# A layer with product-key experts: key rows from a second, transposed copy of peer_u instead of transposes on TensorE

## Chip, cores and metric

The kernel runs on one core of a Trainium2 chip. The metric is the device time of one execution in microseconds; lower is better. Engines are named PE (TensorE), DVE (VectorE), ACT (ScalarE), POOL (GpSimd) and SP (SyncE, which issues most DMAs).

## What is computed

One layer over 1024 latent tokens of width 1024 with 256 context tokens: a modulated norm, an input projection, retention beside differential attention, an output projection, and then a PEER layer, in which every token retrieves experts by product keys. The change lies in the last:

```python
def block_fn(hb):
    q = (hb @ w_query).reshape(t, 8, 2, 128)
    s = einsum('thpc,hpnc->thpn', q, sub_keys)
    v1, i1 = top_k(s[:, :, 0], 16); v2, i2 = top_k(s[:, :, 1], 16)
    cand = v1[..., :, None] + v2[..., None, :]
    best, pos = top_k(cand, 16)                     # 16 of 256 pairs, for each of 8 heads
    experts = i1 * 128 + i2                         # at pos: 128 experts per token, of 16384
    gate = softmax(best)
    act = gelu(einsum('thkd,td->thk', expert_u[experts], hb))
    return einsum('thk,thkd->td', gate * act, expert_v[experts])
```

All data are float32.

## The kernel before

**Two ways through the experts.** The 8 blocks of 128 tokens are split. Blocks 0 to 3 are *gathered*: for each of a token's 128 experts POOL issues an indirect DMA that fetches one 4 KB row of `peer_u` or `peer_v` per token into a `gat` tile (four buffers). `u_step` (from L1212) multiplies the row with the token's h2 on DVE and keeps the sum as a coefficient; `v_step` (L1224) multiplies the row by its coefficient and adds it to `acc` on DVE, or for some ranks scales it on ACT and adds it to `acp` on POOL. That makes 512 u gathers and 512 v gathers. In `halves` (L1208) the u rows of one half block alternate with the v rows of the half before, so that the last 64 v rows come alone.

Blocks 4 to 7 (512 tokens, `DENSE`) take the *dense* part: all 16384 experts for all tokens, with gates that are zero for those not retrieved. `dense_phase` (L1371) goes through 128 key rows of 128 experts, in groups of four. For a key row, `dense_act` (L1315) forms the coefficients: it loads the 128x1024 rows of `peer_u` into `uraw` (tag `wst`, four buffers), transposes them on PE in eight pieces of 128x128 (L1326), and splits the result into a high and a low half, `uh` and `ul` (tag `h`): ACT casts to float32r (L1328) and DVE subtracts what the cast kept from the original (L1329). Three float32r matmuls per piece of the width then give the product with the tokens, which were split in the same way (tags `k` and `v`). After a gelu and the gate (tags `k`, `aT`), the coefficients are split too, and `dense_val` (L1350) multiplies them with the rows of `peer_v` (tag `sel`), whose split has the tags `vi` (cast on ACT) and `pt` (subtraction, on DVE for two of three and on POOL for the third). A group's results are added to `dacc` (tag `b`) on DVE. PSUM has eight banks, all of tag `mm`.

**What sets the order.** No order is written out by hand. `Plan.record` (L208) keeps every instruction with its dependencies, `Plan.cost` (L259) gives it an estimated duration, and `Plan.schedule` (L289) orders all with a list schedule: by priority, and by whether a tile's tag has a free buffer. A priority is the PE time planned so far. `Plan.weave` (L186) sorts several recorded parts together by their position in the list, and `dense_phase` is woven with the last block's selection. The gathers have priorities of their own, a start (`POFF`) and steps per gather (`PACES`), in the same planned PE time:

```python
pr = f0 + POFF
for i, _ in enumerate(halves()):
    nc.prio = pr
    pr += [p for lo, p in PACES if i >= lo][-1]
```

The planned order is then fixed on each engine, and an engine waits for whatever is next in it. Since all instructions are issued from one line (L448), the rows below go by the tiles' names.

Of the kernel before, what the change touches and what calls it, by code (L numbers as in the profile page):

```python
# [14 lines left out]
D = 1024  # L15
# [28 lines left out]
TG = 32  # L44
# [15 lines left out]
class View:  # L60
    """A part of a planned tile: the steps that lead to it, replayed on the real tile when it is traced."""
# [79 lines left out]
class Plan:  # L141
    """Records the kernel's instructions with their data dependencies, orders them with a list schedule on
    estimated durations, and traces them in that order; Tile then places every wait."""
# [35 lines left out]
    def capture(self, fn, *a):  # L179
        """the instructions of fn as a list for weave()"""  # L180
        self._log = log = []
        fn(*a)
        self._log = None
        return log

    def weave(self, *parts):  # L186
        """records captured lists side by side; a part is (list, from, to) with from, to in 0..1"""
        keyed = []
        for x, (log, lo, hi) in enumerate(parts):
            last, key = None, 0.0  # L190
            for j, it in enumerate(log):
                if it[4] is None or it[4] is not last:
                    key = lo + (hi - lo) * j / max(1, len(log))
                last = it[4]
                keyed.append((key, x, j, it))
        keyed.sort(key=lambda z: z[:3])
        for _, _, _, (eng, meth, a, k, u) in keyed:
            if u is None:
                self._in_unit = False
            elif u is not self._token:  # L200
                self._in_unit, self._unit = True, None
            self._token = u
            self.record(eng, meth, a, k)
        self._in_unit, self._unit, self._token = False, None, None
# [84 lines left out]
    def schedule(self):  # L289
# [36 lines left out]
        def blocked(n):  # L326
            """the tag for which the node's tiles have no slot yet, or None"""
            need = {}
            for b in fresh(n):
                need.setdefault(b.tag, []).append(pos[id(b)])  # L330
            for t, ps in need.items():
                bs = self.order[t]
                while head[t] < len(bs) and id(bs[head[t]]) in taken:
                    head[t] += 1
                first = max(ps) < head[t] + len(ps)
                if free[t] < len(ps) + (0 if first else self.reserve.get(t, 99)):
                    return t
            return None
# [116 lines left out]
def layer(tc, I, out, dbg=None):  # L455
# [3 lines left out]
    with sp as S, pp as P, dp as DR:  # L459
# [41 lines left out]
        def rstd(dst, mean):  # L501
            """dst = (mean + eps) ** -0.5 on a narrow tile"""
            n = mean.free
            nc.vector.tensor_scalar(dst, mean, EPS, None, op0=OP.add)
            nc.gpsimd.tensor_tensor(out=dst, in0=dst, in1=mhalf[:, :n], op=OP.pow)

# [82 lines left out]
        def split_cols(kb, xt, tags):  # L589
            """a block's normed, modulated tokens as columns, split in two"""  # L590
# [32 lines left out]
        # log gamma = min(x, 0) - log1p(exp(-|x|)), with log1p(e) = log(u) + (e - (u - 1)) / u, u = 1 + e  # L623
# [15 lines left out]
        # decay columns: [.., a, kind, h], a = forward / backward, kinds k, q, ctx block 0, ctx block 1  # L639
# [17 lines left out]
        # lambda of the differential softmax  # L657
# [9 lines left out]
        # rope tables with the norms' gains in them  # L667
# [13 lines left out]
        def rope(dst, src, cos, sin, g):  # L681
            """dst = src * cos + rot(src) * sin for g groups of 64; src may lie in PSUM"""
# [24 lines left out]
        def three(pm, ah, al, bh, bl, first, last):  # L707
            """pm += (ah + al)^T (bh + bl), each a float32 split in two; the product of the two low parts is below
            float32's last place"""
            nc.tensor.matmul(pm, ah, bh, start=first, stop=False)  # L710
            nc.tensor.matmul(pm, ah, bl, start=False, stop=False)
            nc.tensor.matmul(pm, al, bh, start=False, stop=last)
# [3 lines left out]
        def project3(c0, hs, fn):  # L716
            """256 columns of the input projection, of split tokens"""
# [102 lines left out]
        def late_queries(blocks, tag="rv"):  # L820
            """queries and retention gates of blocks"""
# [11 lines left out]
        # R[:, c] is the state before chunk c in scan order: rows 0:64 forward, rows 64:128 backward  # L833
# [18 lines left out]
        def head_norm(dst, src, gain):  # L852
            """rms over each 128 of 512 columns, times the gain; src in SBUF"""
# [98 lines left out]
        def sub_keys():  # L952
            """the product keys, transposed"""
# [81 lines left out]
        def mix(grp):  # L1035
            """token mixers, output projection and the second norm of up to two blocks; returns h2 of each"""
# [76 lines left out]
        def split_tokens():  # L1113
            """h2 of the dense blocks, transposed and split"""
# [16 lines left out]
        def select(b, v16, i16):  # L1131
# [49 lines left out]
            # per pair of head and rank, on partitions: rows of the two halves' keys and the gate  # L1181
# [26 lines left out]
        def halves():  # L1208
            """the gathered blocks' rows, by half blocks: u rows of one half beside v rows of the half before"""
# [57 lines left out]
        def gates(b):  # L1267
            """gate of expert (i1, i2) for each token of a dense block, into Wd[t // TG][i2][i1][t % TG]; the one-hot
            rows of i1 are products of one-hots of its upper and lower part, those of i2 are relu(1 - |index - column|)"""
# [45 lines left out]
        def dense_act(hhl, i1, wt, j, cs):  # L1315
            """coefficients of the experts of key row i1, for all dense tokens"""
            uraw = sb([128, D], "wst")
            nc.sync.dma_start(uraw, u2[i1 * 128:(i1 + 1) * 128, :])
            uh = sb([128, KD, 128], "h", F32R)
            ul = sb([128, KD, 128], "h", F32R)  # L1320
            for g in range(2):
                tp = ps([128, 4, 128])
                with nc.unit():
                    for q in range(4):
                        k = g * 4 + q
                        nc.tensor.transpose(tp[:, q, :], uraw[:, k * 128:(k + 1) * 128], ident)  # L1326
                ks = slice(g * 4, g * 4 + 4)
                nc.scalar.copy(uh[:, ks, :], tp)  # L1328
                nc.vector.tensor_tensor(out=ul[:, ks, :], in0=tp, in1=uh[:, ks, :].bitcast(F32), op=OP.subtract)  # L1329
# [138 lines left out]

_INS = ["x", "c", "ctx", "c_ctx", "w_mod", "b_mod", "norm1_g", "norm2_g", "w_in", "ret_decay_logit", "ret_norm_g",
# [17 lines left out]
```

## Time and profile before

| | |
|---|---|
| runs (3), median | 3866.08 us (3861.67 to 3867.92) |
| the profiled execution: span from the first to the last instruction | 3853.5 us |
| the profiled execution's own time | not listed apart; it lies among runs whose median is 12.6 us above the span |
| PE, PE weight loads | 3169.3 us (82%), 2518.7 us (65%) |
| DVE | 3019.1 us (78%) |
| ACT | 1429.2 us (37%) |
| POOL | 2283.8 us (59%) |
| moved by DMA | 917.87 MB, 238 GB/s |

Busy times of engines overlap, and a share of the whole span mixes stages: projections and attention in the first half, the dense part beside the gathers in the second. For a change in one stage, the table of that stage (busy times in a stretch), the waits in it, and the chain that ended last say more.

### The profile page before, as it was taken

How to read it: one execution, taken by the hardware profiler on the slowest of the kernel's cores; microseconds unless marked ns; L12 is line 12 of the kernel's file. 1: busy time of each engine (PE TensorE's matmuls, PEld its weight loads, DVE VectorE, ACT ScalarE, POOL GpSimd, SP SyncE). 2: the span in 40 equal slices, each digit the busy share in tenths (PEclk: the TensorE clock that was granted, in tenths of full speed). 3: DMA queues.
4: the chain of work that ended last, by engine and by line, in shares of the span. 5: the costliest groups of instructions: out<-in, count | busy, mean ns of one | idle time of the engine just before them, and what ended most of it. 6: DMA issues, size and time to landing. Idle time of an engine off the chain costs nothing. (4 is left out here: it accounts for less than half of the span.)

```text
span 3853.5 us, 46264 instructions
## 1 busy us (share of the span) xinstructions
PE 3169.3 (82%) x15209; PEld 2518.7 (65%) x15209; DVE 3019.1 (78%) x5843; ACT 1429.2 (37%) x3316; POOL 2283.8 (59%) x1744
## 2 busy tenths in 40 slices
PE   7999998788778658857588898888898888988884
PEld 5998675666556536646476676666677667766663
DVE  3456457788999998999977887787888777778785
ACT  4332424243255447756532233222222222222221
POOL 0111114556765665655677777776777776666677
PEclk9999997889879768867699999999999999999997
DMA  5324464967557657867778888788898888788786
GB/s 179 94 67 130 131 204 148 321 234 248 193 175 253 221 183 238 303 224 245 241 254 286 285 277 274 259 277 279 284 304 292 279 292 277 269 273 274 266 280 214
DMA packets 427392, 917.87 MB, mean 238 GB/s; under 512 B 33384, under 2 KB 224400, under 8 KB 427152
## 3 DMA queue, kind: packets, MB, share of 16 engines
q0 software_dynamic: 147456, 536.94, 41.0%
q1 hardware_dynamic: 279696, 377.98, 29.6%
q8 instruction: 120, 1.97, 0.2%
q14 instruction: 120, 0.98, 0.1%
HBM read 861.84 MB, written 52.95 MB: 237 GB/s over the span
## 5 line engine op out<-in xcount | busy, mean ns | idle before, releaser
L448 DVE SCALAR_TENSOR_TENSOR gat<-gat,h2t 128x1024 f32<-128x1024 f32 x512 | 787.3, 1540 | 177.2 <-DMA gat<-peer_u,egb 174.6
L448 PE MATMUL mm<-k,h 128*128 128x512 f32 x2048 | 748.1, 423 | 142.4 <-DVE h L448 125.1
L448 POOL DMA_INDIRECT gat<-peer_v,egb x512 | 633.3, 1237 | 391.1 <-DVE acc L448 197.4
L448 POOL DMA_INDIRECT gat<-peer_u,egb x512 | 590.6, 1153 | 397.4 <-DVE gat L448 188.5
L448 DVE SCALAR_TENSOR_TENSOR acc<-gat,act,acc 128x1024 f32<-128x1024 f32 x365 | 571.2, 1565 | 111.8 <-DMA gat<-peer_v,egb 111.0
L448 PEld LDWEIGHTS mm<-k,h 128*128 128x128 f32 x2048 | 403.7, 200 | 261.2 <-DVE h L448 150.8
L448 PE MATMUL mm<-v,h 128*128 128x512 f32 x1024 | 421.2, 411 | 0.0
L448 POOL TENSOR_TENSOR acp<-acp,gat 128x1024 f32<-128x1024 f32 x139 | 340.2, 2447 | 64.8 <-ACT gat L448 62.3
L448 PE MATMUL mm<-vi,t 128*128 128x512 f32 x1024 | 355.4, 411 | 0.0
L448 PE MATMUL mm<-vi,rv 128*128 128x512 f32 x1024 | 353.0, 406 | 0.2 <-DVE b L448 0.2
L448 PE MATMUL mm<-o,t 128*128 128x128 f32 x1024 | 201.7, 353 | 177.1 <-DVE o L448 125.9
L448 POOL TENSOR_TENSOR m<-m,mhalf 128x4 f32<-128x4 f32 (+1 forms) x78 | 82.6, 1061 | 406.6 <-DVE m L448 397.8
L448 PEld LDWEIGHTS mm<-o,t 128*128 128x128 f32 x1024 | 174.0, 251 | 214.1 <-issue 60.3
L448 ACT CAST vi<-sel 128x512 fp32r<-128x512 f32 x256 | 158.5, 621 | 389.3 <-PE mm L448 331.0
L448 PE MATMUL mm<-b,wst 128*128 128x256 f32 (+1 forms) x1280 | 266.3, 368 | 3.4 <-ACT t L448 1.7
L448 PE MATMUL mm<-pt,t 128*128 128x512 f32 x512 | 215.4, 421 | 63.0 <-POOL pt L448 32.7
L448 ACT ACTIVATE gat<-gat,act 128x1024 f32<-128x1024 f32 x139 | 160.0, 1151 | 287.0 <-DMA gat<-peer_v,egb 226.7
L448 PE MATMUL mm<-pt,rv 128*128 128x512 f32 x512 | 212.9, 416 | 58.7 <-DVE pt L448 32.5
L448 PEld LDWEIGHTS mm<-b,wst 128*128 128x128 f32 x1280 | 226.1, 213 | 38.9 <-issue 5.2
L448 PEld LDWEIGHTS mm<-vi,t 128*128 128x128 f32 x1024 | 202.5, 198 | 47.2
L448 PEld LDWEIGHTS mm<-v,h 128*128 128x128 f32 x1024 | 204.4, 200 | 42.8
L448 PEld LDWEIGHTS mm<-vi,rv 128*128 128x128 f32 x1024 | 199.6, 195 | 45.3 <-issue 0.4
(249 smaller groups left out, 6620.8 us busy)
## 6 DMA issues: line engine op xcount, KB each, us to landing
wst<-peer_u SPq DMA_DIRECT2D x128, 512.0 KB
sel<-peer_v SPq DMA_DIRECT2D x256, 256.0 KB
wst<-peer_w_query SPq DMA_DIRECT2D x80, 512.0 KB
Wd<-rv SPq DMA_DIRECT2D x64, 512.0 KB
h<-Wd SPq DMA_DIRECT2D x64, 512.0 KB
wst<-w_mod SPq DMA_DIRECT2D x48, 512.0 KB
wst<-w_out SPq DMA_DIRECT2D x40, 512.0 KB
wst<-w_in SPq DMA_DIRECT2D x32, 512.0 KB
```

Of the source, the lines that this page charges most:

```text
L448: getattr(handles[n.eng], meth)(*[res(v) for v in a], **k)
```

## The change

The host adds an input, `peer_u_cols`: for each key row the 128 experts' vectors with the width on the partitions, so that a key row arrives as it left the transposes before. `uraw` is loaded from it, and `uh` and `ul` are made from it in one operation each, of 128x1024 from SBUF in place of two each of 128x512 from PSUM. Matmuls, tags, buffer counts and the planner's constants (`POFF`, `PACES` and the others) stay as they are. The gathers still read `peer_u`.

```diff
         def dense_act(hhl, i1, wt, j, cs):
-            uraw = sb([128, D], "wst")
-            nc.sync.dma_start(uraw, u2[i1 * 128:(i1 + 1) * 128, :])
+            uraw = sb([128, KD, 128], "wst")
+            nc.sync.dma_start(uraw, I["peer_u_cols"][i1])
             uh = sb([128, KD, 128], "h", F32R)
             ul = sb([128, KD, 128], "h", F32R)
-            for g in range(2):
-                tp = ps([128, 4, 128])
-                with nc.unit():
-                    for q in range(4):
-                        k = g * 4 + q
-                        nc.tensor.transpose(tp[:, q, :], uraw[:, k * 128:(k + 1) * 128], ident)
-                ks = slice(g * 4, g * 4 + 4)
-                nc.scalar.copy(uh[:, ks, :], tp)
-                nc.vector.tensor_tensor(out=ul[:, ks, :], in0=tp, in1=uh[:, ks, :].bitcast(F32), op=OP.subtract)
+            nc.scalar.copy(uh, uraw)
+            nc.vector.tensor_tensor(out=ul, in0=uraw, in1=uh.bitcast(F32), op=OP.subtract)
             pm = ps([128, ND])
...
+def host_layouts(inputs):
+    u = np.asarray(inputs["peer_u"])[0].reshape(128, 128, KD, 128)
+    return {"peer_u_cols": np.ascontiguousarray(u.transpose(0, 3, 2, 1))}
...
     arrays.update(shape_constants())
+    arrays.update(host_layouts(inputs))
```

Since the planner sees other steps, it writes another order from the first key row on. On DVE in the middle of the stage, where `h` rows are u splits, `k` and `aT` rows the gating of a key row's coefficients, `gat` and `acc` rows gathers, `pt` rows v splits and `b` rows the sums, the queue read before:

```order
L448 SCALAR_TENSOR_TENSOR gat,act<-gat,h2t 128x1024
L448 TENSOR_TENSOR h<-mm,h 128x512 x3
L448 SCALAR_TENSOR_TENSOR acc<-gat,act,acc 128x1024
L448 TENSOR_TENSOR h<-mm,h 128x512
L448 SCALAR_TENSOR_TENSOR gat,act<-gat,h2t 128x1024
L448 TENSOR_TENSOR pt<-sel,vi 128x512 x2
L448 SCALAR_TENSOR_TENSOR acc<-gat,act,acc 128x1024
L448 TENSOR_TENSOR h<-mm,h 128x512
L448 SCALAR_TENSOR_TENSOR gat,act<-gat,h2t 128x1024 x2
L448 TENSOR_TENSOR k<-k,h 128x256 x2
L448 TENSOR_TENSOR aT<-aT,h 128x256 x2
```

and a like piece of it now:

```order
L448 SCALAR_TENSOR_TENSOR gat,act<-gat,h2t 128x1024
L448 TENSOR_TENSOR h<-wst,h 128x1024
L448 TENSOR_TENSOR k<-k,h 128x256 x2
L448 SCALAR_TENSOR_TENSOR gat,act<-gat,h2t 128x1024
L448 TENSOR_TENSOR h<-wst,h 128x1024
L448 SCALAR_TENSOR_TENSOR acc<-gat,act,acc 128x1024
L448 SCALAR_TENSOR_TENSOR gat,act<-gat,h2t 128x1024
L448 TENSOR_TENSOR aT<-aT,h 128x256 x2
L448 TENSOR_TENSOR pt<-sel,vi 128x512 x2
L448 TENSOR_TENSOR h<-wst,h 128x1024
```

A key row's split is one row instead of two, and splits of several rows stand together: counted over the 128 key rows, a row's split stands on average 2.6 key rows ahead of the gating on DVE, before 1.6. Between two splits there are fewer gathers.

At the end of DVE's queue stood before:

```order
L448 TENSOR_TENSOR pt<-sel,vi 128x512
L448 SCALAR_TENSOR_TENSOR acc<-gat,act,acc 128x1024 x3
L448 TENSOR_TENSOR b<-b,mm 128x512 x2
L448 SCALAR_TENSOR_TENSOR acc<-gat,act,acc 128x1024
L448 TENSOR_TENSOR b<-b,mm 128x512
L448 SCALAR_TENSOR_TENSOR acc<-gat,act,acc 128x1024
L448 TENSOR_TENSOR b<-b,mm 128x512
```

and now:

```order
L448 SCALAR_TENSOR_TENSOR gat,act<-gat,h2t 128x1024 x2
L448 SCALAR_TENSOR_TENSOR acc<-gat,act,acc 128x1024
L448 SCALAR_TENSOR_TENSOR gat,act<-gat,h2t 128x1024
L448 SCALAR_TENSOR_TENSOR acc<-gat,act,acc 128x1024
L448 SCALAR_TENSOR_TENSOR gat,act<-gat,h2t 128x1024
L448 TENSOR_TENSOR act<-act,egb 128x64
L448 SCALAR_TENSOR_TENSOR acc<-gat,act,acc 128x1024 x51
```

Dense work (`pt`, `b`) stood to the last; now the queue ends in gathers alone. Behind DVE's last `b` row there are 19 multiplies of u gathers and 66 accumulations of v gathers. In POOL's queue no gather stood behind the last `pt` split, and now 104 of the 1024 do; the dense blocks' closing operations on POOL (`b<-b,wst`) stand among those.

## Rows read from the trace of the kernel before

**Rows 1.** The page: span; busy us of each engine, share of the span, instructions

```profile
span 3853.5 us, 46264 instructions
...
PE 3169.3 (82%) x15209; PEld 2518.7 (65%) x15209; DVE 3019.1 (78%) x5843; ACT 1429.2 (37%) x3316; POOL 2283.8 (59%) x1744
```

**Rows 2.** Busy by stretch: PE, weight loads, DVE, ACT, POOL, granted clock, DMA share, GB/s

```profile
1885.00:3813.00 1928.00, 1665.70 (x7161) 1311.65 (x7161) 1532.71 (x1855) 551.32 (x880) 1396.49 (x1006) 0.94 0.82 277
```

**Rows 3.** Waits, 1885 to 3813: who waited for whom, us in total, times, longest

```profile
POOL gat L448 <- DVE acc L448: 151.7, 98, 5.5
POOL gat L448 <- DVE gat L448: 151.3, 110, 3.7
...
PE mm L448 <- DVE h L448: 125.1, 47, 13.8
...
POOL gat L448 <- issue: 91.0, 337, 0.6
...
PE mm L448 <- DVE pt L448: 62.3, 32, 6.8
PE mm L448 <- POOL pt L448: 55.7, 33, 6.1
```

**Rows 4.** Tile `gat`, 1885 to 3860: count, ns min/median/max, first and last start

```profile
L448 POOL DMA_INDIRECT gat<-peer_v,egb x376: 935/1118/2016, 1892.0 to 3812.9; - x188
L448 DVE SCALAR_TENSOR_TENSOR gat<-gat,h2t x315: 1208/1225/5019, 1889.7 to 3649.9; 128x1024 f32<-128x1024 f32 x158
...
L448 POOL DMA_INDIRECT gat<-peer_u,egb x313: 935/959/2007, 1886.5 to 3639.6; - x157
L448 DVE SCALAR_TENSOR_TENSOR acc<-gat,act,acc x278: 1267/1282/4328, 1894.7 to 3820.9; 128x1024 f32<-128x1024 f32 x139
```

**Rows 5.** Tiles `wst`, `h` and `pt` in the stage, columns as in the group above

```profile
L448 PEld LDWEIGHTS mm<-ident,wst x1024: 137/141/231, 1885.6 to 3747.8; 128*128 128x128 f32 x171
...
L448 DVE TENSOR_TENSOR h<-mm,h x256: 673/680/697, 1904.0 to 3748.8; 128x512 fp32r<-128x512 f32 x128
...
L448 DVE TENSOR_TENSOR pt<-sel,vi x170: 673/684/4014, 1912.0 to 3808.6; 128x512 fp32r<-128x512 f32 x170
```

**Rows 6.** The page's chain that ended last: share of the span by line

```profile
DMA gat<-peer_v,egb 5%; PE mm L448 4%; POOL gat L448 4%; DMA gat<-peer_u,egb 4%; POOL acp L448 2%; DVE gat L448 1%; POOL pt L448 1%; DVE acc L448 1%; POOL t L448 1%; POOL rv L448 1%; DVE h L448 0%; DVE b L448 0%; POOL b L448 0%; POOL acc L448 0%; ACT gat L448 0%
```

**Rows 7.** Timeline of PE's loads around four transposes: start us, us

```profile
2832.24 0.59 PEld L448 LDWEIGHTS mm<-ident,wst 128*128 128x128 f32 x4
2832.79 0.19 PEld L448 LDWEIGHTS mm<-k,h 128*128 128x128 f32 x1
```

**Rows 8.** Groups by line and form: busy us, mean ns of one, idle before it

```profile
L448 DVE SCALAR_TENSOR_TENSOR gat<-gat,h2t 128x1024 f32<-128x1024 f32 x315 | 519.6, 1650 | 142.7 <-DMA gat<-peer_u,egb 140.1 <-POOL pt L448 1.6 <-issue 0.4
...
L448 DVE SCALAR_TENSOR_TENSOR acc<-gat,act,acc 128x1024 f32<-128x1024 f32 x275 | 434.6, 1580 | 104.0 <-DMA gat<-peer_v,egb 103.2
...
L448 DVE TENSOR_TENSOR h<-mm,h 128x512 fp32r<-128x512 f32 x256 | 169.9, 682 | 24.9 <-ACT h L448 23.5 <-issue 1.0
L448 DVE TENSOR_TENSOR pt<-sel,vi 128x512 fp32r<-128x512 f32 x170 | 164.7, 978 | 26.9 <-ACT vi L448 25.3 <-issue 1.1
...
L448 ACT CAST h<-mm 128x512 fp32r<-128x512 f32 x256 | 141.6, 587 | 134.9 <-PE mm L448 115.6 <-issue 19.1
...
L448 ACT ACTIVATE h<-h,rs 128x1024 f32<-128x1024 f32 x32 | 36.5, 1141 | 0.0
...
L448 DVE TENSOR_TENSOR h<-aT,h 128x1024 fp32r<-128x1024 f32 x8 | 9.8, 1225 | 5.1 <-ACT h L448 5.1
```

**Rows 9.** Groups by form, 3600 to 3780: busy us, mean ns, idle before

```profile
L448 POOL DMA_INDIRECT gat<-peer_v,egb x57 | 70.9, 1244 | 29.2 <-DVE acc L448 17.6 <-issue 7.5 <-POOL acp L448 2.2
...
L448 POOL TENSOR_TENSOR acp<-acp,gat 128x1024 f32<-128x1024 f32 x12 | 28.8, 2396 | 2.2 <-ACT gat L448 1.6 <-DMA gat<-peer_v,egb 0.2
...
L448 POOL DMA_INDIRECT gat<-peer_u,egb x8 | 10.0, 1248 | 9.0 <-DVE gat L448 8.4 <-issue 0.6
```

**Rows 10.** The page's DMA queues: packets, MB, share of 16 engines

```profile
q0 software_dynamic: 147456, 536.94, 41.0%
```

## Prediction, on record before the changed kernel ran

> **What bounds the kernel now.** I read the busy shares first. TensorE (PE) has 82% of the span, VectorE (DVE) 78%, GpSimd (POOL) 59% [rows 1]: no engine is full over the whole, so the stage of the change has to be read by itself. That is the stretch from 1885 us, where the first transposes of key rows start [rows 5], to 3813 us, where the last gather is issued [rows 4]: 1928 us in which PE is busy for 1665.7, DVE for 1532.7 and POOL for 1396.5, at a granted clock of 0.94 and with the DMA engines 82% busy [rows 2]. Two pieces of work run side by side there. The dense part works through 128 key rows, and the gathers fetch one expert row per token each, 376 + 313 = 689 of the 1024 [rows 4]; the other 335 lie earlier. So a key row takes 1928 / 128 = 15.1 us and a gather 1928 / 689 = 2.80 us.
>
> The waits show how the two hold each other. PE stands idle for 1928 - 1665.7 = 262 us; 125 of it is the wait for DVE's half of a u split, 62 and 56 that for DVE's and POOL's v splits [rows 3]. DVE in turn waits 140 and 103 us for gathered rows [rows 8], and POOL waits 152 and 151 us until DVE has given back a gather buffer [rows 3]. DVE takes its work in one fixed order, so a gather that lands late holds up the split queued behind it, and PE then stands. The chain that ended last consists mostly of the gathers: `gat` transfers 5% + 4%, their issue on POOL 4%, `acp` 2%; PE has 4%, and the whole chain covers about 36% of the span [rows 6]. PE is thus the fullest engine, and the gathers are what it is tied to.
>
> **What goes.** Per key row eight transposes. Four of them hold PE from 2832.24 to 2832.79 us [rows 7], so eight cost 1.1 us, and 128 key rows (1024 transposes [rows 5]) 141 us. All of it is on PE, the fullest engine. With them go 256 PSUM banks and the waits of ACT on them (ACT waited 116 us for PE before its u cast [rows 8]); ACT is busy for only 551 of 1928 us [rows 2], so that is worth nothing by itself.
>
> **What is replaced.** ACT: 256 casts of 128x512 from PSUM at 587 ns (150 us) become 128 of 128x1024 from SBUF, near the 1141 ns of another 128x1024 on ACT [rows 8], 146 us. Nothing. DVE: 256 subtractions from PSUM at 682 ns (175 us) become 128 of 128x1024 with both inputs in SBUF. The same form took 1225 ns in the quiet part at the start [rows 8]. In the stage, operations with two SBUF inputs run longer: the gathers' multiplies have a minimum of 1208 and a mean of 1650 ns, their accumulations 1267 and 1580, the v splits 673 and 978 [rows 4, 5, 8], while the subtraction from PSUM never left 673 to 697 ns [rows 5]. So the new one costs between 1.225 us (157 us in all, a gain of 18) and 1.65 us (211, a loss of 36). I take 1.6, near the multiplies, which have its size: 205 us, DVE loses 30.
>
> By the Trainium skill, page "VectorE: DVE Perf Modes", section on the TRN2 errata, an operation from SBUF takes 58 cycles beside its elements and one from PSUM 120; at 0.96 GHz that would make 1.13 us of the new one and 1.32 of the two old ones, a gain of some 24 us over 128 rows, by which DVE would be busy in the stage some 54 us less than I reckon below. The quiet 1225 ns already lies above that, and the stage's rows further, so I go by the rows.
>
> DMA: the load of a key row stays 512 KB in one issue, one contiguous 4 KB piece per partition as before. Nothing.
>
> **What moves.** The planner lays out the dense part in fewer steps, and that shifts it against the gathers. Up to the first u split every engine's order is the same. After it, a key row carries fewer gathers: behind the last v split in POOL's queue stand 104 of the 1024 gathers where none stood before, and DVE's queue ends in 51 accumulations with no dense work between them. So a stage with 689 - 104 = 585 gathers is followed by a tail of 104. Second, DVE's u splits stand 2.6 key rows ahead of the product of their row's coefficients, where it was 1.6 (mean over the 128).
>
> **The sum**, in parts of the span of 3853.5 us:
>
> - Before the stage: 1885, unchanged.
> - The stage. PE's work falls to 1665.7 - 141 = 1525. Its idle time of 262 us can at worst stay; at best the whole goes at the gathers' own pace, 585 x 2.80 = 1638 us, which leaves PE 113 idle. I let two thirds of the 125 us that PE waited for u splits go (84), since splits stand a key row earlier and DVE meets 15% fewer gathers in between, and keep the rest: 178. The stage is 1703 us, between 1638 and 1787. DVE would be busy there for 1532.7 + 30 less the 19 multiplies and 66 accumulations that leave for the tail (some 136), 1427 us or 84%, against 79% now: possible, but with less room.
> - The tail of 104 gathers. No slower than in the stage (2.80 us; the last stretch had 57 + 8 in 180 us, 2.77 [rows 9]). No faster than the DMA engines: the gathers' queue used 41.0% of the span [rows 10], 0.41 x 3853.5 / 1024 = 1.54 us each. POOL needs, for five v gathers and one addition, 5 x (1.24 + 0.3 of issue) + 2.4 = 10.1 us [rows 3, 9], 2.0 each, and four buffers never keep it supplied without a gap: I take 2.2, so 229 us, between 160 and 291.
> - The end. Now 40.6 us lie behind the last gather's issue [rows 4], with eight multiplications and additions of the dense blocks among those of the last gathered block. These now come before; most ran while the gathered block's own loads were on their way, so I take off three, at the 2.4 us of an addition of that size [rows 9]: 33.
>
> 1885 + 1703 + 229 + 33 = 3850, against 3853.5. The runs' median of 3866.1 lies 12.6 above the span; on that scale the forecast is **3863 us**. 141 us of PE's work go and 84 us of its waits, and the tail, in which PE has nothing to do, takes the gain back. A difference under 0.2% (8 us) can't be told from none here. The balance turns where the stage is 3853.5 - 1885 - 229 - 33 = 1706 us, that is where PE loses 81 us of its idle time.
>
> **Rival 1, slower: DVE takes over as the bound.** The subtraction leaves the one kind of DVE operation that POOL never delayed (673 to 697 ns) for the kind that stretched to 4 and 5 us [rows 4, 5]; the delay falls on whatever is queued behind it, gathers' multiplies and v splits, and POOL then waits longer for buffers. If for this PE keeps its 262 us of idle time, the stage is 1787 us, and the end 1885 + 1787 + 229 + 33 = 3934, a time of 3947. For it: DVE's share rises to 84%, and 118 us of PE's waits are for v splits, which have only two buffers and stand no earlier than before. Against it: nearly half of PE's idle time was the wait for just those u splits that now stand earlier. It decides as soon as less than 81 us of the 262 go.
> The Trainium skill, page "GPSIMD Engine Reference", section "Key points", says that GpSimd shares its SBUF interfaces with VectorE and contends with DVE instructions that have two SBUF inputs. The rows above agree with that; by it the chance of this case would be higher than I put it, since the split now belongs to that kind in every key row.
>
> **Rival 2, faster: the gathers set the pace of the stage.** For it: the chain, where they have the larger part. Then the stage shrinks with their number to 1638 us, and the span is 1885 + 1638 + 229 + 33 = 3785, a time of 3798. Against it: PE would have to be busy for 1525 of 1638 us, 93%, where it reached 86%.
>
> **Rival 3: it does nothing of the kind**, because the new array's loads come late. The bytes, the pieces and the place in SP's queue are the same; and no wait of PE for them stands among the longer ones. 1 in 50; at the price of Rival 1, since PE would then keep its idle time, some 3950 us.
>
> **How the numbers follow.** The forecast's case, 3835 to 3890, has 0.40; Rival 1, 3890 to 3960, 0.33; Rival 2, 3790 to 3835, 0.25; Rival 3, 0.02. The tail's bounds (160 to 291) add some 20 us at either end. The range 3780 to 3945 leaves out less than 2 in 10: a stage at the gathers' pace with a fast tail below, a full Rival 1 above. The forecast's own range is 3835 to 3890. Faster by over 0.2% (below 3858): all of Rival 2 and 0.16 of the forecast's case, 0.41. Within 0.2%: 0.17 of that case. Slower: the rest, 0.42.
>
> **What would show it.** Right: no transposes of `wst`; the new subtraction at about 1.6 us; PE's wait for DVE's `h` at about 40 us instead of 125; the last matmul near 1885 + 1703 = 3590 us; behind it only gathers, at 2.2 us. Wrong, if the wait for `h` stays above 100 us or that for `pt` grows by what the other lost (Rival 1), if the last matmul comes before 3540 (Rival 2), or if the tail runs at 2.8 us or at 1.6. That a tail exists is the surest part, since it stands in the queues.

## The result and the profile after

The changed kernel takes 3899.36 us (median of 4 runs, 3896.57 to 3919.0) against 3867.0 us of the kernel before beside it (3861.67 to 3875.68): a ratio of 1.009, 95% interval [1.0061, 1.0118]. It is slower by 32 us. That lies inside the range of 3780 to 3945, but the forecast, no clear difference, did not hold.

The page of the kernel after, span and busy times (to [rows 1]):

```profile
span 3894.9 us, 44031 instructions
...
PE 3027.8 (78%) x14185; PEld 2398.6 (62%) x14185; DVE 3036.2 (78%) x5715; ACT 1413.8 (36%) x3188; POOL 2348.7 (60%) x1744
```

PE lost 141.5 us of work (3169.3 to 3027.8), as predicted, and the span grew by 41.4 us. Where it grew is read from first and last starts. Tiles `h`, `pt` and `gat` after (to [rows 4, 5]; count, ns min/median/max, first and last start):

```profile
L448 DVE TENSOR_TENSOR h<-wst,h x128: 1206/1216/5055, 1912.7 to 3514.0; 128x1024 fp32r<-128x1024 f32 x128
```

```profile
L448 DVE TENSOR_TENSOR pt<-sel,vi x170: 674/682/3628, 1924.3 to 3597.6; 128x512 fp32r<-128x512 f32 x170
L448 POOL TENSOR_TENSOR pt<-sel,vi x86: 1255/1305/2285, 1927.7 to 3608.5; 128x512 fp32r<-128x512 f32 x86
```

```profile
L448 POOL DMA_INDIRECT gat<-peer_v,egb x376: 932/1167/2015, 1904.3 to 3865.7; - x188
```

| piece of the span | before | after | difference |
|---|---|---|---|
| to DVE's first u split | 1904.0 | 1912.7 | +8.7 |
| from there to DVE's last v split | 1904.6 | 1684.9 | -219.7 |
| from there to the last gather's issue | 4.3 | 268.1 | +263.8 |
| from there to the end | 40.6 | 29.2 | -11.4 |

The four differences make the 41.4 us. (The first piece holds no changed code. After's profiled execution took 3896.68 us, 1.8 more than its span; if before's stood so too, it lay some 11 us under its median, and between the medians the difference is 32.) So the dense stage became 220 us shorter, and the tail of gathers gave back more.

Busy times after, by stretch (columns as in [rows 2]): the stage, the tail, the end.

```profile
1897.00:3614.00 1717.00, 1524.24 (x6147) 1192.84 (x6148) 1413.03 (x1623) 518.77 (x735) 1303.74 (x890) 0.95 0.82 280
3614.00:3866.00 252.00, 0.98 (x3) 0.26 (x1) 140.57 (x110) 18.61 (x17) 176.37 (x126) 0.51 0.67 226
3866.00:3895.00 29.00, 0.00 (x0) 0.00 (x0) 5.24 (x3) 1.15 (x1) 9.98 (x5) 0.50 0.29 105
```

PE is busy for 1524.2 of 1717 us, 89%: its idle time is 193 us, where 178 were forecast. In the tail PE has nothing to do. Waits after, 1897 to 3614 (to [rows 3]):

```profile
POOL gat L448 <- DVE gat L448: 138.0, 104, 4.6
...
POOL gat L448 <- DVE acc L448: 86.1, 66, 4.0
PE mm L448 <- DVE pt L448: 79.4, 42, 5.6
...
PE mm L448 <- POOL pt L448: 74.4, 32, 6.4
...
PE mm L448 <- DVE h L448: 31.3, 16, 14.9
```

PE's wait for u splits fell from 125 to 31 us (forecast: 40), and that for v splits rose from 118 to 154.

The tail by itself, timeline of the kernel after (start us, us, engine, operation, count, idle before and what ended it):

```profile
3769.80 2.34 POOL L448 TENSOR_TENSOR acp<-acp,gat 128x1024 f32<-128x1024 f32 x1 [1.28 <-ACT gat L448]
3770.72 5.14 DVE L448 SCALAR_TENSOR_TENSOR acc<-gat,act,acc 128x1024 f32<-128x1024 f32 x3 [3.40 <-DMA gat<-peer_v,egb]
3773.49 1.88 POOL L448 DMA_INDIRECT gat<-peer_v,egb  x1 [1.35 <-DVE acc L448]
3775.67 0.99 POOL L448 DMA_INDIRECT gat<-peer_v,egb  x1 [0.31 <-issue]
3776.97 0.94 POOL L448 DMA_INDIRECT gat<-peer_v,egb  x1 [0.30 <-issue]
3778.22 0.94 POOL L448 DMA_INDIRECT gat<-peer_v,egb  x1 [0.30 <-issue]
3778.82 1.28 DVE L448 SCALAR_TENSOR_TENSOR acc<-gat,act,acc 128x1024 f32<-128x1024 f32 x1 [2.96 <-DMA gat<-peer_v,egb]
3780.37 0.94 POOL L448 DMA_INDIRECT gat<-peer_v,egb  x1 [1.22 <-DVE acc L448]
3780.93 1.15 ACT L448 ACTIVATE gat<-gat,act 128x1024 f32<-128x1024 f32 x1 [11.21 <-DMA gat<-peer_v,egb]
3782.16 2.34 POOL L448 TENSOR_TENSOR acp<-acp,gat 128x1024 f32<-128x1024 f32 x1 [0.85 <-ACT gat L448]
```

The cut lies where only v gathers are left. From one addition to `acp` to the next are 12.36 us for five gathers, 2.47 each. POOL first waits for ACT's scaling of the row that its addition needs (1.28, 0.85), adds it, and only then issues; twice more it waits for DVE to give back a buffer (1.35, 1.22). 104 gathers lie behind POOL's last v split at 3608.5, and they take 257 us. Among the first 41 of them (20 u and 21 v gathers) POOL also does the dense blocks' eight closing operations:

```profile
L448 POOL TENSOR_TENSOR b<-b,wst 128x1024 f32<-128x1024 f32 x8 | 19.8, 2479 | 0.1
```

So 20 of the 257 us are dense work; the last 63 gathers, v rows alone, are issued from 3714.1 to 3865.7, 2.45 us apart.

### The profile page after: what moved, and what is told of

It is laid out like the page before. It is cut to its first block, busy times and chain, and to the rows that moved or that the text cites. A ratio compares the mean times of both kernels' runs of the same rounds, so it can differ in the third digit from the quotient of the medians.

```text
span 3894.9 us, 44031 instructions
## 1 busy us (share of the span) xinstructions
PE 3027.8 (78%) x14185; PEld 2398.6 (62%) x14185; DVE 3036.2 (78%) x5715; ACT 1413.8 (36%) x3188; POOL 2348.7 (60%) x1744
## 5 line engine op out<-in xcount | busy, mean ns | idle before, releaser
L448 POOL DMA_INDIRECT gat<-peer_v,egb x512 | 658.8, 1287 | 363.5 <-DVE acc L448 161.9
L448 POOL DMA_INDIRECT gat<-peer_u,egb x512 | 617.6, 1206 | 394.8 <-DVE gat L448 174.4
L448 PE MATMUL mm<-k,h 128*128 128x512 f32 x2048 | 678.0, 399 | 35.1 <-DVE h L448 31.3
L448 PEld LDWEIGHTS mm<-k,h 128*128 128x128 f32 x2048 | 387.4, 190 | 140.1 <-DVE h L448 40.0
L448 PE MATMUL mm<-v,h 128*128 128x512 f32 x1024 | 409.6, 400 | 0.0
L448 DVE TENSOR_TENSOR h<-wst,h 128x1024 fp32r<-128x1024 f32 x128 | 192.3, 1507 | 43.1 <-ACT h L448 43.1
```

Of the source, the lines that this page charges most:

```text
L448: getattr(handles[n.eng], meth)(*[res(v) for v in a], **k)
```

## The experiments

Each run stands beside runs of the kernel before on the same chip; "+23 us" is the difference of the two medians, the bracket the 95% interval of the ratio. The question behind them: whose work sets the pace of the dense stage? Where a diff shows the trace loop, the planned order stays what it was, and only what is issued differs.

**1. The transposes alone, in the order of before.** The changed kernel was planned as if the transposes were still there, and they were then left out (E1) or issued all the same, into PSUM that nobody reads (E2). So the splits are of 128x512 from SBUF, and no tail arises.

```diff
+            for g in range(2):
+                tp = ps([128, 4, 128])
+                ks = slice(g * 4, g * 4 + 4)
+                tp.base.alias = uraw[:, ks, :]
...
+                nc.vector.tensor_tensor(out=ul[:, ks, :], in0=tp, in1=uh[:, ks, :].bitcast(F32), op=OP.subtract)
...
+                    dead = meth == "transpose" and a[0].base.alias is not None
+                    if dead:        # E1 only
+                        continue
```

> The transposed copy and no transposes, but planned as if the transposes were still there: the order of the kernel before, u splits in two halves of 128x512 from SBUF, no tail of gathers (5 of 1024 stand behind the last v split instead of 104). Tail theory (the change lightens the stage and loses it again because its new order leaves 104 gathers for the end): faster than before, by some 60 to 120 us, 3745 to 3805, the last gather issued within 20 us of the last matmul. Rival (the split from SBUF loads DVE and its contention with POOL, which costs what PE saves): 3850 to 3900, with PE's idle time in the stage at 300 us or more instead of 262.

> As e1_order_kept, but the 1024 transposes are still issued on PE, into PSUM tiles that nobody reads; the split is made from the loaded copy in SBUF. It separates PE's time for transposes (against e1) from the split's change of source (against the kernel before). Tail theory: 3860 to 3890, near before, since only the split's source differs, and some 100 us above e1. Rival (the split's source is what costs): 3900 or more, above the kernel before by 40 us or more, and e1 less than 60 us below it.

Measured: E1 3886.19 us, +23 [1.0041, 1.0078]; E2 3871.79 us, +9 [1.0001, 1.0033]. E1 lies in the range of its rival and 80 us above that of the tail theory; E2 lies in the tail theory's range by itself, but not 100 us above E1, so neither account holds. The tail was not what ate the gain: without a tail, and without the 141 us of transposes on PE, E1 is no faster than before. E1 by stretch, and what PE waited for in the stage:

```profile
1898.00:3825.00 1927.00, 1588.06 (x6133) 1220.67 (x6133) 1567.54 (x1848) 551.05 (x878) 1419.74 (x1000) 0.91 0.82 276
```

```profile
PE mm L454 <- DVE h L454: 179.1, 64, 14.5
POOL gat L454 <- DVE acc L454: 153.8, 102, 5.3
POOL gat L454 <- DVE gat L454: 138.0, 109, 3.8
```

The stage lasts 1927 us as it did before (1928). PE is busy for 78 us less and waits 54 us longer for the u splits; POOL's waits for buffers stay at 292 us (303 before). DVE's splits from SBUF cost 60 us more than from PSUM in E1 (group by form: 230.0 us at a mean of 919 ns, against 169.9 at 682 [rows 8]). E2, which has those as well (229.2 us at a mean of 916 ns), is 9 us above the kernel before, so they explain little. Why E1 lies above E2, with less to do, stays open; over the stage (1898 to 3830 in E2) PE waited 136 us for u splits in E2 at a granted clock of 0.94, in E1 179 us at 0.91.

**2. The tail's length.** The planner's steps per gather are multiplied by 0.8 (E3) and 0.9 (E4), so that more gathers come ahead of the stage (434 and 383 ahead of POOL's first v split) and 15 and 64 instead of 104 remain behind it.

```diff
-POFF, PACES = -16.6, [[0, 1.9], [300, 1.73], [600, 1.18], [1000, 1.9], [1500, 1.9]]
+POFF, PACES = -16.6, [[0, 1.52], [300, 1.384], [600, 0.944], [1000, 1.52], [1500, 1.52]]
```

> The changed kernel with the five steps of PACES times 0.8: gathers are planned earlier, 434 of them before the first v split on POOL instead of 344, and 15 behind the last instead of 104. Tail theory: the 89 gathers leave a tail where each took 2.47 us (220 us) for a place beside other work where one costs 1 to 2 us: 3740 to 3810. Rival (gathers cost the same wherever they stand, DVE and POOL being the bound throughout): 3870 to 3910, the stretch before the first v split some 220 us longer.

> As e3_pace80 with the steps times 0.9: 383 gathers before the first v split, 64 behind the last. Tail theory: about half of the gain of e3_pace80, 3810 to 3860. Rival: 3880 to 3910.

Measured: E3 3844.70 us, -18 [0.9915, 0.9994]; E4 3874.07 us, +11 [1.0008, 1.0041]. E3's stage starts 160 us later than after's and is as long (2073.0 to 3767.1, 1694 us, against 1685): 89 gathers cost some 1.8 us each ahead of the stage, and 2.47 in the tail. So the tail is only a dear place for gathers. Both times lie between the ranges of the two theories: against the kernel before E3 gained some 50 us on the changed kernel, where the tail theory asked for about 90 or more.

**3. PE's and DVE's work in the stage.** From E1's order the matmuls with the low half of the key rows are left out (E5), then DVE's subtractions that make it too (E6).

```diff
+                    if dead or meth == "matmul" and a[1].base.low or meth == "tensor_tensor" and k["out"].base.low:    # E5: without the last
+                        continue
...
+            ul.base.low = True
```

> The order of before with the transposed copy and without transposes (e1), and now also without the 1024 matmuls of the tokens' high half with the low half of a key row (ul), which are an eighth of a key row's PE work at about 0.23 us each; ul is still computed, and the product is left out of the result. Theory A, the gathers' path (issue on POOL, landing, DVE's use, the buffer's return) sets the pace of the stage and PE follows: no change against e1, 3875 to 3895 us, and PE's idle time in the stage grows by about 230 us. Theory B, PE's work sets the pace wherever it is busy and e1 lost its gain only through the longer wait for the split from SBUF: most of 230 us is gained, 3650 to 3760 us.

> As e5, and the subtractions that make ul are left out as well, so that DVE loses 256 operations of 919 ns, 235 us of its 1577 in the stage of e1; the low half of peer_u's key rows is left out of the result. Theory A, the latency of the loop of four gather buffers sets the pace: DVE's work counts only as far as it stands between a row's landing and its use, a small gain, 3830 to 3880 us. Theory C, DVE is the bound and all its work counts: 3650 to 3720 us, PE and DVE both idle more or DVE's share stays near 81%.

Measured: E5 3872.57 us, +8 [0.9987, 1.0040]; E6 3870.04 us, +6 [0.9987, 1.0034]. E6 by stretch:

```profile
1897.00:3813.00 1916.00, 1385.69 (x5109) 1063.13 (x5109) 1380.51 (x1592) 541.38 (x877) 1373.98 (x999) 0.85 0.81 277
```

PE is down to 72% of the stage and DVE to 72%, and it lasts 1916 us. PE's busy time is 202 us less than in E1 and the kernel 15 us faster; E6 takes another 186 us off DVE's (1566.4 in E5) for 3 us, each give or take some 10 us by the intervals. Neither engine is the bound, though they are the two fullest. That speaks against Rival 1's reason as much as against the forecast's.

**4. One more gather buffer.** Every fifth gather, from the 400th (E7, E12) or the 520th (E8) on, goes to a tile in an idle slot of tag `v`; the order on the engines stays. E7 is E1 with it, E8 is E3, E12 the kernel before.

```diff
+            if b.tag == "gat":
+                ngat[0] += 1
+                if ngat[0] >= 400 and ngat[0] % 5 == 0:
+                    if not spare:
+                        spare.append(S.tile([128, D], F32, name="gat5", tag="v", bufs=bufs["v"]))
+                    return spare[0]
```

> e1 with exactly its order on every engine, but every fifth gather from the 400th on goes to a fifth tile (a slot of the tag v that stands idle then) in place of one of the four gat buffers. Theory A, the loop of four buffers (about 2.8 us x 4 = 11 us from a gather's issue to the next use of its buffer) sets the pace of the stage: with five it could fall to 2.2 us a gather until another limit is met, so clearly faster than e1's 3886, 3700 to 3840 us, and POOL waits less for DVE's gat and acc. Theory C, DVE or POOL's own work sets the pace: no change, 3870 to 3895 us.

> e3 (the changed kernel with the gathers' steps in the planner times 0.8, 3845 us) with the same order, and a fifth gather tile for every fifth gather from the 520th on. Theory A: the stage of e3 (1714 us) shortens towards PE's work, 3700 to 3810 us in all. Theory C: no change, 3835 to 3855 us.

> The kernel before in its exact order with the transposes, and the fifth gather tile of e7. If the 1024 transposes cost nothing beside the gathers even with the fifth buffer, it comes to the time of e7 less the dearer subtraction's share, 3800 to 3830 us (e7: 3832). If PE's work begins to count once buffers are no longer short, it gains less than e7 did against e1: 3830 to 3860 us.

Measured: E7 3832.32 us, -32 [0.9875, 0.9939], 55 us under E1; E8 3800.79 us, -64 [0.9790, 0.9873], 45 under E3; E12 3827.32 us, -37 [0.9878, 0.9926]. E7 and E8 lie in theory A's ranges, at their slow ends, and E12 in the range of its first case. POOL's waits for buffers in E7, 1900 to 3783:

```profile
POOL gat L454 <- issue: 127.4, 481, 1.8
...
POOL gat L454 <- DVE acc L454: 59.6, 36, 8.7
...
POOL gat L454 <- DVE gat L454: 26.6, 28, 5.5
```

They fall from 292 to 86 us, and the stage by 46 (1914.8 to 3776.6 on DVE's splits, against 1912.4 to 3820.1 in E1). The buffers count, but they are not the whole: most of what POOL no longer waits for, it waits for elsewhere (before the dense part's operations 116 us in place of 48, before additions to `acp` 66 in place of 32). And E12, with all its transposes, is as quick as E7 without them.

**5. The transfers beside the gathers.** E1 without the loads of key rows; casts and subtractions read a resident tile.

```diff
+                    if dead or meth == "dma_start" and isinstance(a[0], View) and a[0].base.held is not None:
+                        continue
...
             nc.sync.dma_start(uraw, I["peer_u_cols"][i1])
+            uraw.base.held = held[0]
...
                 nc.sync.dma_start(vraw, v2[i1 * 128:(i1 + 1) * 128, hs])
+                vraw.base.held = held[1]
```

> e1 in its exact order, but the 128 loads of key rows of peer_u and the 256 of peer_v (134 MB, a quarter of what the DMA engines move in the stage) are left out; the casts and subtractions of the same size read a resident tile of the tokens instead, so the dense part's result is another. Theory A, the gathers' loop of buffers sets the pace, whose time from issue to landing shrinks with less traffic (6 us beside the loads): 3820 to 3870 us. Theory D, the transfers themselves (DMA engines 82% busy) set the pace: the stage could fall by up to a quarter, 3450 to 3700 us. Theory E, work on POOL and DVE in the order they stand sets it: no change, 3870 to 3890.

Measured: 3818.21 us, -46 [0.9849, 0.9915], 69 under E1. DVE's wait for u rows and the stretch (1897 to 3765):

```profile
DVE gat L454 <- DMA gat<-peer_u,egb: 65.6, 52, 7.5
```

```profile
1897.00:3765.00 1868.00, 1570.99 (x6131) 1214.48 (x6131) 1550.81 (x1843) 547.91 (x872) 1404.25 (x998) 0.92 0.67 213
```

The time lands just under theory A's range. DVE's wait for u rows falls from 131 us in E1 to 66 and the DMA share from 0.82 to 0.67, so the gathers land sooner without the loads; but a quarter of the bytes buys 1.8%, so the transfers are not the bound.

**6. POOL's own work.** POOL adds the rows that ACT has scaled to `acp`, in the same queue that issues the gathers. In E10 these additions read `acp` twice, so that the row's buffer is free earlier; in E11 they are left out. Both have E1's order.

```diff
+                    if meth == "tensor_tensor" and n.eng == "POOL" and k["out"].base.tag == "acp" and k["in1"].base.tag == "gat":
+                        k["in1"] = k["in0"]          # E10; E11: continue
```

> e1 in its exact order; POOL's additions to acp (139 in all, some 95 in the stage at 2.4 us) take acp itself as second input instead of the gathered row, so POOL works as long, but a gathered row's buffer is free once ACT has scaled it, and POOL waits for ACT no more; acp's part of the gathered blocks is another. Theory A (buffers' loop): faster than e1 by 20 to 80 us. Theory E (POOL's busy time): within 15 us of e1's 3886.

> As e10, but the additions to acp are left out altogether (POOL loses some 330 us of work over the kernel, some 230 in the stage). Theory A: no more than e10 gains, or 20 us more. Theory E, POOL's work in its order sets the pace: 100 to 230 us faster than e10, 3640 to 3780 us.

Measured: E10 3828.16 us, -36 [0.9878, 0.9941]; E11 3692.86 us, -171 [0.9514, 0.9560]. E10 does not tell what it should: the addition itself became shorter (1973 ns in the mean for 2566), so POOL lost 55 us of work in the stage beside the wait. E11 is plain: 135 us under E10, 194 under E1, which is what theory E asked for and theory A excluded. POOL's groups in the stage of E11 (busy us, mean ns, idle before and what ended it), and its stretch:

```profile
L456 POOL DMA_INDIRECT gat<-peer_v,egb x371 | 465.7, 1255 | 371.3 <-DVE acc L456 238.2 <-ACT gat L456 48.7 <-issue 44.6
L456 POOL DMA_INDIRECT gat<-peer_u,egb x313 | 346.3, 1106 | 236.5 <-DVE gat L456 110.6 <-issue 47.3 <-DMA gat<-peer_v,egb 37.7
```

```profile
1854.00:3663.00 1809.00, 1548.09 (x6133) 1197.93 (x6133) 1417.26 (x1848) 550.19 (x877) 1140.31 (x906) 0.93 0.86 294
```

334 us of POOL's work over the kernel (139 x 2.4) bring 194 us; now POOL waits more for DVE to return buffers. PE's work (E5) and DVE's splits (E6) did not count like this; ACT's was not tried. The 194 us are not POOL's queue alone: without the additions DVE's operations on gathered rows became shorter too (501.6 to 433.8 us for the u rows, 415.7 to 396.2 for the v rows, E1 to E11), and they stand in the same ring. How the 194 us divide between the two was not tested.

**7. Moving that work instead of leaving it out.** E13 is E8 with every row added on DVE, and E13 to E16 and E18 are planned anew, so their order changes too. E14 keeps POOL's rows in the first two half blocks and a sixth of the third; E15 has the steps x 0.9; E16 is the kernel before with the edits of E13; E18 is E16 with the steps of before.

```diff
-VPAT = ['PDDPDD', 'PDD', 'PDDPDD', 'PDPDD', 'PDDDD']
+VPAT = ['D']
+VPAT = ['PDDPDD', 'PDD', 'PDDDDD', 'DDDDD', 'DDDDD']      # E14
```

> e8 (changed kernel, gathers' steps x 0.8, fifth gather tile; 3801 us) with every v row added on DVE: no scaling on ACT and no addition on POOL (139 of 512 rows before), nothing left out. POOL loses 139 x 2.4 = 334 us of work over the kernel, DVE gains 139 x 1.3 = 181. Theory F (POOL's queue, in which the additions stand ahead of gathers, sets the pace, and DVE has room): 3640 to 3740 us. Theory G (DVE, 82% busy, is the next bound and takes it back): 3780 to 3850 us.

> As e13, but the first two gathered blocks' early halves keep POOL's share, and only the half blocks that run in the dense stage give theirs to DVE. Theory F: between e13 and e8, near e13, 3660 to 3760 us. Theory G: near e8.

> As e13 with the gathers' steps x 0.9: 50 gathers fewer ahead of the dense stage and 31 more behind it, at some 2 us each beside the dense part and 2.5 behind it: within 30 us of e13, rather slower.

> The kernel before, with transposes, and the same three edits as e13. Theory F with PE free as long as gathers are the slower side: within 30 us of e13. If PE's 141 us of transposes begin to count once the gathers are quicker: 60 to 140 us slower than e13.

E17 puts 1024 dead transposes back into E13.

```diff
+                    if meth == "matmul" and a[0].base.idle:
+                        row, eye = a[0].base.idle
+                        a[0].base.idle = None
+                        for q in range(8):
+                            c = slice(q % 4 * 128, q % 4 * 128 + 128)
+                            self.nc.tensor.transpose(res(a[0][:, c]), res(row[:, c]), res(eye))
...
+            pm.base.idle = hhl[0][0].bitcast(F32), ident
```

> e13 (3685 us) in its exact order, with 1024 transposes put back on PE as dead work: eight ahead of each key row's first matmul, of a resident tile, into the bank that those matmuls then overwrite. PE gets back 141 us of work and nothing else changes. PE is 92% busy in the stage of e13. If PE's work counts there: 60 to 150 us slower, 3745 to 3835 us. If the 239 us between e16 and e13 come from the other order (in e16 the gathers end 315 us before the dense part): within 40 us of e13.

> e16 (the kernel before, with transposes, no additions on POOL, fifth gather tile) with the steps of before in place of x 0.8, so that the gathers end nearer to the dense part's end (7 v splits behind the last gather in POOL's queue, against 19). If the order made e16 slow: 3700 to 3800 us, with the transposes' 141 us as the rest against e13. If PE's work does by itself: above 3850 us.

| | median us | to before | interval of the ratio |
|---|---|---|---|
| E13 | 3685.36 | -184 | [0.9484, 0.9562] |
| E14 | 3698.63 | -170 | [0.9514, 0.9595] |
| E15 | 3675.33 | -194 | [0.9465, 0.9558] |
| E16 | 3924.37 | +55 | [1.0107, 1.0188] |
| E17 | 3704.23 | -157 | [0.9564, 0.9623] |
| E18 | 3796.01 | -65 | [0.9783, 0.9841] |

E13, E14 and E18 lie in the ranges of theory F or the first case, E15 came out 10 us quicker where rather slower was expected, and E16 fits neither of its cases. DVE takes 139 additions more, and the kernel becomes faster. E15 is the quickest that was run, 4.9% under the kernel before and 5.7% under the changed one (3675.33 / 3899.36). E16 looked at first as if the transposes were worth 239 us. They are not: E17 puts the same work on PE in E13's order, and costs 26 us (each taken against the kernel before beside it), within the 40 of its second case. The stages of E13 and E17 by stretch:

```profile
2020.00:3660.00 1640.00, 1482.97 (x6126) 1168.10 (x6127) 1430.32 (x1695) 435.95 (x655) 1140.84 (x825) 0.96 0.87 299
```

```profile
2009.00:3672.00 1663.00, 1565.50 (x7142) 1260.52 (x7142) 1426.95 (x1695) 436.20 (x654) 1157.50 (x825) 0.98 0.86 295
```

PE goes from 90% to 94% busy and the stage grows by 23 us, with 141 us of transposes in it. What E16 lacked, for the larger part, was the balance of the gathers and the dense part, as its gathers and v splits show:

```profile
L448 POOL DMA_INDIRECT gat<-peer_v,egb x332: 932/958/2012, 2016.4 to 3568.0; - x166
```

```profile
L448 POOL TENSOR_TENSOR pt<-sel,vi x86: 1267/1294/2342, 2037.9 to 3883.5; 128x512 fp32r<-128x512 f32 x86
```

The last gather is issued 315 us before the last v split. E18, with the gathers laid out later, takes 121 us off. It still lies 118 us above E13; how much of that another order would take off, and how much the transposes cost in this order, was not tried.

## Why the prediction was wrong

**What failed** is its first step on the sum, "PE's work falls to 1665.7 - 141 = 1525. Its idle time of 262 us can at worst stay", with the stage as PE's work plus a part of its idle time. E1 shows that the stage does not follow PE: the 141 us of transposes went, PE's idle time rose from 262 to 339 us, past what "can at worst stay", and the stage stayed at 1927 us. The forecast read 86% busy as the bound and the waits as friction on it. The profile of before held the answer in a view that was not weighed, POOL's groups by form in the same stretch (columns as in [rows 8]):

```profile
L448 POOL DMA_INDIRECT gat<-peer_v,egb x376 | 476.7, 1268 | 257.5 <-DVE acc L448 151.7 <-DVE gat L448 45.5 <-issue 40.7
L448 POOL DMA_INDIRECT gat<-peer_u,egb x313 | 362.7, 1159 | 179.1 <-DVE gat L448 105.8 <-issue 50.3 <-DMA gat<-peer_v,egb 5.0
L448 POOL TENSOR_TENSOR acp<-acp,gat 128x1024 f32<-128x1024 f32 x94 | 231.0, 2458 | 38.2 <-ACT gat L448 36.2 <-DMA gat<-peer_v,egb 0.6 <-issue 0.4
L448 POOL TENSOR_TENSOR pt<-sel,vi 128x512 fp32r<-128x512 f32 x85 | 121.7, 1432 | 8.5 <-ACT vi L448 7.3
L448 POOL TENSOR_TENSOR t<-k,t 128x512 fp32r<-128x512 f32 x32 | 48.8, 1526 | 6.1 <-ACT t L448 5.1 <-issue 0.6
L448 POOL TENSOR_TENSOR rv<-aT,rv 128x512 fp32r<-128x512 f32 x32 | 45.7, 1427 | 15.2 <-ACT rv L448 14.5 <-issue 0.3
L448 POOL TENSOR_TENSOR rv<-k,rv 128x512 fp32r<-128x512 f32 x32 | 45.5, 1422 | 13.8 <-ACT rv L448 13.4
L448 POOL TENSOR_TENSOR t<-aT,t 128x512 fp32r<-128x512 f32 x32 | 45.0, 1407 | 8.3 <-ACT t L448 7.1 <-issue 0.9
```

POOL works for 1396.5 us. Of its 532 us of idle time, 437 stand before gathers and 38 before additions to `acp`; for the dense part (the last five rows) it waits 52 us. The least busy of the three engines hardly ever waits for the dense part, while PE's idle time is nearly all waits for DVE and POOL. By itself this is a reading; the runs bear it out (E5 and E6 against PE and DVE as the bound, E7, E12 and E11 for the ring): the gathers' path (POOL's queue, the landing, DVE's use, the buffer's return) sets the pace, and the dense part follows.

Point by point, by the prediction's own steps:

- *Before the stage, the loads, ACT*: they held; the first piece moved by 8.7 us with no changed code in it.
- *The subtraction at 1.6 us*: 1.507 in the mean (192.3 us for 128), on the side that was taken; E6 shows that its size made little difference. The 1.13 us that the prediction worked out from the Trainium skill, page "VectorE: DVE Perf Modes", section on the TRN2 errata, lie under the minimum of 1.206 here; the same section says that the figure of 58 cycles comes out too low and gives (N + 151) / 0.96 ns for a float32 `tensor_tensor` of N elements, an estimate of 1.224 us, with which the median of 1.216 agrees.
- *The stage at 1703 us*: 1717 in the stretch shown. The number is near by luck, the reason was wrong: 141 us of PE's work and 84 of its waits make 225, and the stage shrank by 219.7. But in E1, where all gathers stay in it, the stage did not shrink at all; here 102 of its 689 gathers left it (587 are in the stretch after), 2.15 us each. No run puts the transposes back into the changed kernel's own order; E1, and E17 in a third order, stand for it.
- *The tail of 104 gathers at 2.2 us*: 2.47, so 257 us for 229. 20 of the 28 us more are the dense blocks' eight closing operations, which the prediction moved ahead of the end and took off there in part, but put at nothing in the tail. For the rest, the sum had POOL's five issues and one addition and 0.9 us of gaps in five gathers; in the cycle shown POOL's wait for ACT's scaling (0.85) and its two waits for buffers (1.35 and 1.22) follow one another and make 3.4, while the issues were shorter than reckoned.
- *The end at 33 us*: 29.2.

In span the sum missed by 45 us (3850 against 3895): 12 ahead of the stage, 14 in it, 23 in the tail by the stretches above (252 against 229), less 4 at the end.

A gather thus costs 2.15 us beside the dense part and 2.47 in the tail. The pieces of the table behind the first give the change: 264 us more of tail, less 220 of stage, less 11 at the end make +33 us, and 32 lie between the medians. That PE's 141 us have no place in that sum rests on E1 and E17.

**Rival 1** gave the right sign, and the time lies in its range of 3890 to 3960, for a reason that fell: PE's wait for v splits did grow, by 36 us, but its wait for u splits fell by 94, and DVE is not the bound (E6). **Rival 2** had the right mechanism, with the wrong price: 2.80 us per gather holds POOL's work for the dense part as well. The rows above let it be split: 306.7 us of such work and 51.9 us of waits before it leave 1928 - 359 = 1569 us for 689 gathers, 2.28 each; with the same dense work 585 gathers would have made a stage of 1692 us, not 1638. With the tail at 2.47, which only the result gives, this rival would have forecast 1885 + 1692 + 257 + 33 = 3867 us of span, 13 us slower than before and the right way.

## What to carry to other kernels

Before crediting an engine's saved work, ask who never waits for it: here an engine that was 86% busy and spent the rest waiting was a follower, and the pace was set by the queue whose waits close in a ring among themselves (issue, landing, use, buffer's return), at 72% busy. A stage that shrinks because work was moved out of it has not become faster; price the moved work where it now stands, with every wait in its cycle and all else that moved there with it. Work that shared a queue with the gathers was dear: additions moved from POOL to the fuller DVE, with a new order, brought 3% (E13 against E8), while the eight transposes of every key row cost 26 us where that was tested (E17).

## What the runs showed of the hardware

- POOL's additions lengthened DVE's operations from SBUF. In E11, with the same 1848 instructions on DVE in the stage as E1, DVE is busy for 1417.3 us in place of 1567.5: the 93 additions had cost DVE 1.6 us each. The Trainium skill, page "GPSIMD Engine Reference", section "Key points", names such contention with DVE instructions of two SBUF inputs; the trace agrees, and the size is this case's.
- A 128x1024 addition on POOL took 1973 ns in the mean where both inputs were the same tile, and 2566 with two different ones (E10 and E1).
- PE's clock fell where it idled more, so that part of what was taken from PE came back as slower work: its mean granted clock (full is 2.4 GHz, the lower level 1.2) over the stage was 0.94 before, with 262 us idle, 0.91 in E1 with 339 and 0.85 in E6 with 530, and 0.98 in E17 with 97. In E1 PE's busy time fell by 78 us where 141 us of transposes had gone.
